# Gate and up by one level of Strassen's scheme, down in four parts, score products in pairs

## The chip, the cores and the metric

The kernel runs on one core of one Trainium2 chip. The metric is the device time of one execution in microseconds, the median over several. The engines are TensorE (matrix products; PE in the profile, PEld its weight loads), VectorE (DVE), ScalarE (ACT), GpSimd (POOL) and SyncE (SP), which issues the loads. DMA engines move data between memory and the on-chip buffers.

## The reference

Four feed-forward layers, one attention and one gating mixer (gMLP) act on x of 512 tokens by 1024, in float32:

```
def _swiglu_ffn(x, w_gate_up, w_down):
    g, u = jnp.split(x @ w_gate_up, 2, axis=-1)
    return (jax.nn.silu(g) * u) @ w_down
...
    for i in range(DEPTH):                       # DEPTH = 2, D_FF = 2816
        x = x + 0.5 * _swiglu_ffn(_rmsnorm(x, ffn1_norm[i]), ffn1_w_gate_up[i], ffn1_w_down[i])
        h = _rmsnorm(x, mix_norm[i])
        # i = 0: x = x + _diff_attention(h, ...)   8 heads of two components, 64 wide
        # i = 1: x = x + _chunked_sgu(h, ...)
        x = x + 0.5 * _swiglu_ffn(_rmsnorm(x, ffn2_norm[i]), ffn2_w_gate_up[i], ffn2_w_down[i])
```

## The kernel before

x stays on the chip as eight tiles of 128 features by 512 tokens (k = 0 to 7). The feed-forward layers are f0 to f3, the norms n0 to n5; the order is f0, attention, f1, f2, gMLP, f3. A float32 product is made of three float32r products (`mm3`, L126 to L129): each operand is split into a high half (ScalarE's copy, L122 for weights) and a low half (VectorE's subtraction, L123), and high times high, high times low and low times high are added in one bank.

A feed-forward layer has 22 tiles of 128 hidden features, in two halves of 11. For a tile one load brings 1 MB (gate and up, 256 columns for each k), two splits of 1024 columns follow, and 8 k times 2 sides times 3 products of 512 tokens fill two banks. The normalisation is applied behind the products: x is only multiplied by the norm's gain (L158, L159), and the row `rb` of 1/rms multiplies the banks in `gated` (L235 to L243), which then takes silu on ScalarE, multiplies, and splits the result into the tiles hh and hl. `rb` is made by `norm.rstd` and `norm.rows` from sums that TensorE takes during the first tile (in f0 the second). After 11 tiles `down` runs: for each of the eight output tiles m one load of 704 KB, two splits, 33 products, and x[m] += 0.5 times the bank (L285). In the second half each finished x[m] goes at once into the next norm.

Four buffers hold weights that are loaded or being loaded in feed-forward and mixers alike (`wraw` two of 2048 columns, `wsplit` five pairs of 1024). A scheduler orders each engine's instructions by need and cost; attention and gMLP first put their tasks in order by a planner of their own (`interleave`), with due times. In attention the score products of a head and row (L495) come in two components of 64 features, each with its own bank, three products and a mask product (L499); they are spread between the products of values (v0p and on).

Of the kernel before, what the change touches and what calls it, by code (L numbers as in the profile page):

```python
# [43 lines left out]
DOWN_CUT = 6  # L44
O_BUFS = 4
U_BUFS = 4
QK_BUFS = 5
BANKS = {"pp": 4, "ps": 3, "po": 1}
HOP = 0.2
# [4 lines left out]
def kernel(  # L54
# [28 lines left out]
    wraw = ctx.enter_context(tc.tile_pool(name="wraw", bufs=2))  # L83
    wsplit = ctx.enter_context(tc.tile_pool(name="wsplit", bufs=5))
# [7 lines left out]
    xh = [acts.tile([P, S], F32R, name=f"xh{k}") for k in range(KT)]  # L92
    xl = [acts.tile([P, S], F32R, name=f"xl{k}") for k in range(KT)]
# [49 lines left out]

    class Norm:


        def __init__(self, layer, kind, name):
            self.g0 = C_GAIN + (layer * 3 + kind) * KT
            self.name = name
            self.acc = stat.tile([P, S], F32, tag="sqacc", name=name + "acc", bufs=1)  # L150

# [17 lines left out]
        def rstd(self):  # L169

            ps = bank(self.name + "ss", "po")
            for n in range(NT):
                nc.tensor.matmul(
                    ps[:, n:n + 1], self.acc[:, n * P:(n + 1) * P], ones[:, 0:1], start=True, stop=True
                )
# [4 lines left out]
        def rows(self, r):  # L180
# [6 lines left out]
            for part, half in ((f32(rh), "h"), (rl, "l")):  # L187
# [37 lines left out]

    def ffn(layer, which, norm, nxt):
        f = layer * 2 + which
        nm = f"f{f}"
        with ExitStack() as c:
            hp = c.enter_context(tc.tile_pool(name=nm + "h", bufs=1, reuse_waits="tile"))  # L230
            tp = c.enter_context(tc.tile_pool(name=nm + "t", bufs=2, reuse_waits="tile"))

            def gated(j, jj, ps):
                gt = tp.tile([P, S], F32, tag="gt", name=f"{nm}g{j}")
                nc.vector.tensor_tensor(gt, ps[0], rb, op=ALU.mult)  # L235
                nc.scalar.activation(gt, gt, AF.Silu)
                ut = tp.tile([P, S], F32, tag="ut", name=f"{nm}u{j}")
                nc.vector.tensor_tensor(ut, ps[1], rb, op=ALU.mult)
# [620 lines left out]
```

## Time and profile before

| | |
|---|---|
| median of 3 runs | 1996.73 us (1996.42 to 1997.2) |
| profiled execution | 1996.96 us, its span 1995.2 us |
| TensorE busy | 1984.2 us, 99%, 9034 products |
| its weight loads | 1629.9 us, 82% |
| VectorE busy | 1032.3 us, 52% |
| ScalarE busy | 670.0 us, 34% |
| DMA | 190.34 MB, mean 95 GB/s |

Busy is the time in which an engine has at least one instruction in work; products overlap, so a product's duration is longer than the step from its start to the next one's. What an instruction costs a full engine is therefore read as the step between starts.

### The profile page before, as it was taken

What the parts mean: (1) busy time and instruction counts of PE and PEld (TensorE: products, weight loads), DVE (VectorE), ACT (ScalarE), POOL (GpSimd) and SP (SyncE); (2) the same over time, 40 slices, a digit from 0 to 9 for tenths busy, and PEclk for the clock granted to TensorE, in tenths of its full rate; (3) what the DMA queues carried; (4) which work ended last, traced back from release to release, by engine and by line L of the source; (5) the groups of instructions that cost most, each with busy time, mean ns of one, the idle gap of its engine ahead of it and who ended that gap; (6) DMA issues with size and microseconds to landing.
All of it is one profiled execution on the core that took longest, in us unless ns stands there. A gap on an engine that the chain in (4) does not pass through costs nothing.

```text
span 1995.2 us, 22193 instructions
## 1 busy us (share of the span) xinstructions
PE 1984.2 (99%) x9034; PEld 1629.9 (82%) x9034; DVE 1032.3 (52%) x1663; ACT 670.0 (34%) x960; POOL 2.6 (0%) x11
## 2 busy tenths in 40 slices
PE   8999999999999999999999999999999999999999
PEld 7888888877778888888888888888888888888887
DVE  7433444567778443444544334445586564434442
ACT  5222323355554322222423223233333242222321
POOL 0000000000000000000000000000000000000000
PEclk9999999999999999999999999999999999999999
DMA  5223222211112222322322232234332222223222
GB/s 193 99 73 120 100 86 94 105 64 64 55 52 85 89 81 95 126 84 74 127 87 90 88 127 85 79 103 146 115 116 85 89 102 88 83 94 127 85 78 81
DMA packets 32934, 190.34 MB, mean 95 GB/s; under 512 B 3776, under 2 KB 4160, under 8 KB 16576
## 3 DMA queue, kind: packets, MB, share of 16 engines
q1 hardware_dynamic: 32832, 188.93, 27.0%
q8 instruction: 71, 1.16, 0.2%
q14 instruction: 31, 0.25, 0.0%
HBM read 186.82 MB, written 2.10 MB: 95 GB/s over the span
## 4 chain that ended last, share of the span: by engine, by line
PE 98%; DVE 1%; ACT 1%; DMA 0%; SPq 0%; issue 0%; ACTq 0%
PE f2p L127 4%; PE f3p L127 4%; PE f3p L128 4%; PE f2p L129 4%; PE f3p L129 4%; PE f2p L128 4%; PE f1p L127 4%; PE f1p L128 4%; PE f1p L129 4%; PE f0p L127 4%; PE f0p L129 4%; PE f0p L128 4%; PE f3dp L127 2%; PE f2dp L129 2%; PE f1dp L127 2%; PE f0dp L129 2%
## 5 line engine op out<-in xcount | busy, mean ns | idle before, releaser
L235 DVE TENSOR_TENSOR f3g<-f3p,n5rbs 128x512 f32<-128x512 f32 x22 | 15.2, 691 | 58.7 <-PE f3p L129 58.7
L235 DVE TENSOR_TENSOR f1g<-f1p,n2rbs 128x512 f32<-128x512 f32 x22 | 15.2, 692 | 58.7 <-PE f1p L129 57.3
L235 DVE TENSOR_TENSOR f2g<-f2p,n3rbs 128x512 f32<-128x512 f32 x22 | 15.2, 691 | 58.7 <-PE f2p L129 58.7
L235 DVE TENSOR_TENSOR f0g<-f0p,n0rbs 128x512 f32<-128x512 f32 x22 | 15.2, 691 | 55.5 <-PE f0p L129 55.5
L158 ACT ACTIVATE xh<-x,sm 128x512 fp32r<-128x512 f32 x48 | 34.3, 718 | 17.8 <-DVE x L750 9.7
L159 DVE SCALAR_TENSOR_TENSOR xl<-x,sm,xh 128x512 fp32r<-128x512 f32 x48 | 35.6, 746 | 8.5 <-ACT xh L158 8.4
L285 DVE SCALAR_TENSOR_TENSOR x<-f3dp,x 128x512 f32<-128x512 f32 x16 | 11.1, 692 | 40.3 <-PE f3dp L129 40.3
L285 DVE SCALAR_TENSOR_TENSOR x<-f2dp,x 128x512 f32<-128x512 f32 x16 | 11.1, 692 | 29.3 <-PE f2dp L129 29.3
L285 DVE SCALAR_TENSOR_TENSOR x<-f1dp,x 128x512 f32<-128x512 f32 x16 | 11.1, 692 | 29.3 <-PE f1dp L129 29.3
L285 DVE SCALAR_TENSOR_TENSOR x<-f0dp,x 128x512 f32<-128x512 f32 x16 | 11.1, 692 | 29.3 <-PE f0dp L129 29.3
L750 DVE TENSOR_TENSOR x<-gop,x 128x512 f32<-128x512 f32 x24 | 16.5, 689 | 18.4 <-PE gop L129 18.4
L242 ACT ACTIVATE f3hh<-f3u 128x512 fp32r<-128x512 f32 x22 | 13.9, 633 | 28.1 <-DVE f3u L239 28.1
L242 ACT ACTIVATE f2hh<-f2u 128x512 fp32r<-128x512 f32 x22 | 13.9, 632 | 28.0 <-DVE f2u L239 28.0
L243 DVE TENSOR_TENSOR f3hl<-f3u,f3hh 128x512 fp32r<-128x512 f32 x22 | 15.2, 692 | 15.4 <-ACT f3hh L242 15.4
L243 DVE TENSOR_TENSOR f2hl<-f2u,f2hh 128x512 fp32r<-128x512 f32 x22 | 15.2, 692 | 15.4 <-ACT f2hh L242 15.4
L242 ACT ACTIVATE f1hh<-f1u 128x512 fp32r<-128x512 f32 x22 | 13.9, 632 | 27.3 <-DVE f1u L239 27.3
L243 DVE TENSOR_TENSOR f1hl<-f1u,f1hh 128x512 fp32r<-128x512 f32 x22 | 15.2, 692 | 14.7 <-ACT f1hh L242 14.7
L242 ACT ACTIVATE f0hh<-f0u 128x512 fp32r<-128x512 f32 x22 | 13.9, 632 | 26.5 <-DVE f0u L239 26.5
L593 DVE TENSOR_TENSOR x<-aop,x 128x512 f32<-128x512 f32 x32 | 21.5, 684 | 2.4 <-PE aop L129 2.3
L243 DVE TENSOR_TENSOR f0hl<-f0u,f0hh 128x512 fp32r<-128x512 f32 x22 | 15.2, 692 | 14.1 <-ACT f0hh L242 14.0
L730 ACT ACTIVATE gh<-gut 128x512 fp32r<-128x512 f32 x16 | 10.1, 631 | 33.7 <-DVE gut L729 33.7
L689 DVE TENSOR_TENSOR gut<-gup,n4rbs 128x512 f32<-128x512 f32 x16 | 11.0, 685 | 13.4 <-PE gup L129 13.4
(3643 smaller groups left out, 6456.7 us busy)
## 6 DMA issues: line engine op xcount, KB each, us to landing
f1gu<-in_gate_up_dram SPq DMA_DIRECT2D x22, 1024.0 KB, 4.8
f2gu<-in_gate_up_dram SPq DMA_DIRECT2D x22, 1024.0 KB, 4.8
f3gu<-in_gate_up_dram SPq DMA_DIRECT2D x22, 1024.0 KB, 4.8
f0gu<-in_gate_up_dram SPq DMA_DIRECT2D x21, 1024.0 KB, 4.8
f0d<-in_down_dram SPq DMA_DIRECT2D x16, 704.0 KB, 4.0
f1d<-in_down_dram SPq DMA_DIRECT2D x16, 704.0 KB, 4.0
f2d<-in_down_dram SPq DMA_DIRECT2D x16, 704.0 KB, 4.1
f3d<-in_down_dram SPq DMA_DIRECT2D x16, 704.0 KB, 4.1
```

Of the source, the lines that this page charges most:

```text
L127: nc.tensor.matmul(ps, sh, mh, start=start, stop=False)
L128: nc.tensor.matmul(ps, sh, ml, start=False, stop=False)
L129: nc.tensor.matmul(ps, sl, mh, start=False, stop=stop)
L158: nc.scalar.activation(xh[k], x[k], AF.Copy, scale=g)
L159: nc.vector.scalar_tensor_tensor(xl[k], x[k], g, f32(xh[k]), op0=ALU.mult, op1=ALU.subtract)
L235: nc.vector.tensor_tensor(gt, ps[0], rb, op=ALU.mult)
L242: nc.scalar.activation(a, ut, AF.Copy)
L243: nc.vector.tensor_tensor(b, ut, f32(a), op=ALU.subtract)
L285: nc.vector.scalar_tensor_tensor(x[m], pt, 0.5, x[m], op0=ALU.mult, op1=ALU.add)
L593: nc.vector.tensor_tensor(x[m], pt, x[m], op=ALU.add)
L689: nc.vector.tensor_tensor(ut, ps, rr["rb"], op=ALU.mult)
L750: nc.vector.tensor_tensor(x[m], pt, x[m], op=ALU.add)
```

## The change

Tiles are taken in pairs, i and i + 11. Tiles 0, 11, 1 and 12 stay as they were (PLAIN = 2); the other nine pairs are done by one level of the Winograd form of Strassen's scheme over (first or second tile) by (first or second half of k) by (first or second 256 tokens): seven products of half the k and half the tokens instead of eight. Each product is done for gate (a) and for up (b), so a pair has 14 turns of 4 k times 3 products of 256 columns, in the order of `turns`, on three accumulators X, Y, Z for each side; `keep` holds what is copied out between.

The weights are four quarters, each a load of 512 KB: a, b (tiles i and i + 11, first half of k), d, c (the same, second half). VectorE makes t = a + b, then t + c once t is split for Q5; two more sums are made by DMAs from GpSimd's queue that load a quarter from memory a second time and add it into the buffer: b += c as soon as t is made, t += d as soon as t + c is split for P6. The last, t + d + c, is split for Q4. All seven weight operands are split as before. `scaled` makes the seven combinations of x once per layer, now with gain and `rb` both multiplied in, and splits them.

Down takes its 22 hidden tiles in four parts (CHUNKS), each when its pairs are done, with two loads and one split of up to 768 columns for each m, and adds to x[m] four times. All products of a feed-forward layer are kept in the program's order. Each norm's xh and xl come from a pool shared with the hidden tiles. Attention has 4 instead of 5 buffers for q and k, gMLP 3 instead of 4 for u, and the score products of a group, save the first, and their masks are kept in program order, the two components alternating.

```diff
-U_BUFS = 4
-QK_BUFS = 5
+U_BUFS = 3
+QK_BUFS = 4
...
+HT = S // 2
+PLAIN = 2
+C_BUFS = 1
+CHUNKS = ((0, 1, 2), (3, 4, 5), (6, 7, 8), (9, 10))
...
+    pairs = ctx.enter_context(tc.tile_pool(name="pairs", bufs=10))
+    wraw = ctx.enter_context(tc.tile_pool(name="wraw", bufs=4))
+    wsplit = ctx.enter_context(tc.tile_pool(name="wsplit", bufs=4))
     psum = ctx.enter_context(tc.tile_pool(name="psum", bufs=8, space=bass.MemoryType.PSUM))
...
+    fixed = []
+
+    def matmul(ps, stationary, moving, start, stop, more=False):
+
+        mm = nc.tensor.matmul(ps, stationary, moving, start=start, stop=stop, skip_group_check=more)
+        if fixed:
+            tc.keep_in_program_order(mm)
+
+    def mm3(ps, sh, sl, mh, ml, start, stop, more=False):
...
+    class Weigh:
+        def __init__(self, pool, srcs, name):
+            self.name, self.done, self.srcs = name, {}, srcs
+            self.raw = {}
+            for q in "abdc":
+                if q == "c":
+                    t = pool.tile([P, 1024], F32, tag="c", name=f"{name}c", bufs=C_BUFS)
+                else:
+                    t = wraw.tile([P, 1024], F32, tag="raw", name=f"{name}{q}")
+                self.raw[q] = t
+                nc.sync.dma_start(t, srcs[q])
+            t = self.raw["t"] = pool.tile([P, 1024], F32, tag="t", name=f"{name}t", bufs=2)
+            nc.vector.tensor_tensor(t, self.raw["a"], self.raw["b"], op=ALU.add)
+            self.more("b", "c")
+        def more(self, to, by):
+            nc.gpsimd.dma_start(self.raw[to], self.srcs[by], accum_op=ALU.add)
+        def take(self, prod):
+            if prod not in self.done:
+                src = {"P1": "a", "Q5": "t", "P6": "t", "P7": "b", "P2": "d", "Q3": "c", "Q4": "t"}[prod]
+                self.done[prod] = split(self.raw[src], D, self.name + prod)
+                if prod == "Q5":
+                    t = self.raw["t"]
+                    nc.vector.tensor_tensor(t, t, self.raw["c"], op=ALU.add)
+                elif prod == "P6":
+                    self.more("t", "d")
+            return self.done[prod]
...
+        slot = {"P1": 0, "P2": 1, "Q4": 2, "Q5": 3, "P6": 4, "P7": 5, "Q3": 6}
+        turns = ["P1a", "P1b", "Q5a", "P6a", "P6b", "Q5b", "P7a", "P7b", "P2a", "P2b", "Q3a", "Q3b", "Q4a", "Q4b"]
...
+            def gated(j, ps):
+                h = room(f"{nm}r{j}")
+                g, u = h[:, :2, :], h[:, 2:4, :]
+                nc.vector.tensor_tensor(g, two(ps[0]), two(rb), op=ALU.mult)
+                nc.scalar.activation(g, g, AF.Silu)
+                nc.vector.tensor_tensor(u, two(ps[1]), two(rb), op=ALU.mult)
+                nc.vector.tensor_tensor(u, u, g, op=ALU.mult)
+                late_halves.append((j, u))
+            def scaled(kp):
+                h = room(f"{nm}x{kp}")
+                for k, dst in ((kp, h[:, 0:8:7, :]), (kp + 4, h[:, 1:3, :])):
+                    nc.vector.scalar_tensor_tensor(
+                        dst, two(x[k]), norm.gain(k), two(rb), op0=ALU.mult, op1=ALU.mult
+                    )
+                nc.vector.tensor_tensor(h[:, 3, :], h[:, 7, :], h[:, 2, :], op=ALU.subtract)
+                nc.vector.tensor_tensor(h[:, 4, :], h[:, 3, :], h[:, 0, :], op=ALU.subtract)
+                nc.vector.tensor_tensor(h[:, 5, :], h[:, 0, :], h[:, 7, :], op=ALU.subtract)
+                nc.vector.tensor_tensor(h[:, 6, :], h[:, 1, :], h[:, 4, :], op=ALU.add)
+                hi, lo = (
+                    fp.tile([P, 7, HT], F32R, tag="x" + q, name=f"{nm}x{kp}{q}", bufs=4) for q in "hl"
+                )
+                nc.scalar.activation(hi, h[:, :7, :], AF.Copy)
+                nc.vector.tensor_tensor(lo, h[:, :7, :], f32(hi), op=ALU.subtract)
+                xf.append((hi, lo))
+            late_halves = []
+            plain = [j for i in range(PLAIN) for j in (i, i + FH)]
...
+                late.append((j, ps))
+                if at == 1:
+                    for unit in late:
+                        gated(*unit)
+                    late = []
+            for kp in range(4):
+                scaled(kp)
+            for unit in late:
+                gated(*unit)
+            for unit in late_halves:
+                halves_of(*unit)
+            def gate_up_pair(i):
+                quarter = lambda j, q: gate_up[f, j][:, q * D:(q + 1) * D]
+                weigh = Weigh(
+                    fp, {"a": quarter(i, 0), "b": quarter(i + FH, 0), "c": quarter(i + FH, 1), "d": quarter(i, 1)},
+                    f"{nm}w{i}",
+                )
+                h = room(f"{nm}r{i}")
+                g, h = h[:, :4, :], h[:, 4:, :]
+                keep, acc = {}, {}
+                for turn in turns:
+                    prod, u = turn[:2], turn[2]
+                    wh, wl = weigh.take(prod)
+                    home = {"P2": "Z", "Q4": "X"}.get(prod, {"P": "X", "Q": "Y"}[prod[0]])
+                    fresh = prod in ("P1", "P2", "Q5")
+                    if fresh:
+                        acc[home + u] = bank(f"{weigh.name}{home}{u}", "ps" if home == "X" else "pp")
+                    ps = acc[home + u][:, :HT]
+                    for k, (hi, lo) in enumerate(xf):
+                        c0 = slice((k * 2 + (u == "b")) * P, (k * 2 + (u == "b") + 1) * P)
+                        mm3(
+                            ps, wh[:, c0], wl[:, c0], hi[:, slot[prod], :], lo[:, slot[prod], :],
+                            fresh and k == 0, k == 3, not fresh,
+                        )
+                    out = g if u == "a" else h
+                    if prod in ("P1", "P6", "P7"):
+                        if prod == "P1":
+                            keep[u] = fp.tile([P, 2, HT], F32, tag="keep" + u, name=f"{nm}k{i}{u}")
+                        if prod == "P7":
+                            kept = fp.tile([P, HT], F32, tag="keep", name=f"{nm}k{i}{u}")
+                        else:
+                            kept = keep[u][:, ("P1", "P6").index(prod), :]
+                        nc.scalar.activation(kept, ps, AF.Copy)
+                    if prod == "P7":
+                        nc.vector.tensor_tensor(out[:, 3, :], acc["Y" + u][:, :HT], kept, op=ALU.subtract)
+                    elif prod == "P2":
+                        nc.vector.tensor_tensor(out[:, 0, :], ps, keep[u][:, 0, :], op=ALU.add)
+                        if u == "a":
+                            nc.scalar.activation(g[:, 0, :], g[:, 0, :], AF.Silu)
+                        else:
+                            nc.vector.tensor_tensor(h[:, 0, :], h[:, 0, :], g[:, 0, :], op=ALU.mult)
...
+            def down_part(chunk):
+                k0, n = chunk[0], len(chunk)
+                js = [i + q * FH for q in range(2) for i in chunk]
...
+            for i in range(PLAIN, FH):
+                gate_up_pair(i)
+                for chunk in CHUNKS[:-2]:
+                    if i == chunk[-1] + 1:
+                        down_part(chunk)
+            down_part(CHUNKS[-2])
+            down_part(CHUNKS[-1])
+            fixed.pop()
...
-                        nc.tensor.matmul(
+                        mm = nc.tensor.matmul(
                             pss[cc][:, :L], qT[a][c0, i * P:L], kT[b][c0, :L], start=(a + b == 0), stop=False
                         )
+                        if a + b + cc > 0:
+                            tc.keep_in_program_order(mm)
                 for cc in range(2):
-                    nc.tensor.matmul(pss[cc][:, i * P:L], ident_b, mask_b, start=False, stop=True)
+                    tc.keep_in_program_order(
+                        nc.tensor.matmul(pss[cc][:, i * P:L], ident_b, mask_b, start=False, stop=True)
+                    )
                 for cc in range(2):
```

VectorE at the entry of f1, before. f1g and f1u are the two sides of a gated tile, f1w31l the low half of a weight split, n2rbs the norm row.

```order
L235 TENSOR_TENSOR f1g_5349<-f1p_5267,n2rbs 128x512 [waits Activation_49]
L238 TENSOR_TENSOR f1u_5352<-f1p_5268,n2rbs 128x512
L239 TENSOR_TENSOR f1u_5352<-f1u_5352,f1g_5349 128x512 [waits DVE_49,Activation_49]
L123 TENSOR_TENSOR f1w31l<-f1gu_5499,f1w31h 128x1024 [waits PE_49,Activation_49]
L243 TENSOR_TENSOR f1hl_5356<-f1u_5352,f1hh_5355 128x512 [waits Activation_49]
L235 TENSOR_TENSOR f1g_5419<-f1p_5369,n2rbs 128x512 [waits PE_49]
L238 TENSOR_TENSOR f1u_5422<-f1p_5370,n2rbs 128x512 [waits PE_49]
L123 TENSOR_TENSOR f1w40l<-f1gu_5569,f1w40h 128x1024 [waits DMAHW0_49,Activation_49]
```

VectorE at the same place after the norm row, now: f1x are the combinations of x, x1 to x3 those of k pairs 1 to 3, f1w2 the first pair's weights, f1r the gating of a plain tile.

```order
L325 SCALAR_TENSOR_TENSOR f1x_6737<-x_84,sm,n2rbs 128x512
L330 TENSOR_TENSOR f1x_6737<-f1x_6737 128x256 [waits DVE_49]
L328 TENSOR_TENSOR f1x_6737<-f1x_6737 128x256 [waits DVE_49]
L273 TENSOR_TENSOR f1w2t<-f1w2t,f1w2c 128x1024 [waits DMAHW7_49]
L336 TENSOR_TENSOR f1x2l<-f1x_6726,f1x2h 128x1792 [waits Activation_49]
L329 TENSOR_TENSOR f1x_6737<-f1x_6737 128x256 [waits DVE_49]
L315 TENSOR_TENSOR f1r_6748<-f1p_6592,n2rbs 128x512 [waits DVE_49]
L331 TENSOR_TENSOR f1x_6737<-f1x_6737 128x256 [waits DVE_49]
L317 TENSOR_TENSOR f1r_6748<-f1p_6593,n2rbs 128x512
L126 TENSOR_TENSOR f1w2P6l<-f1w2t,f1w2P6h 128x1024 [waits PE_49,Activation_49]
L318 TENSOR_TENSOR f1r_6748<-f1r_6748 128x512 [waits DVE_49,Activation_49]
L336 TENSOR_TENSOR f1x3l<-f1x_6737,f1x3h 128x1792 [waits Activation_49]
```

Where only gating and weight splits stood, the combinations of x, the sum of two weight quarters and the gating of plain tiles now stand in turn, and the low half of the last combination (x3l) comes last.

VectorE in one pair of f2 with the next one's start, now (f2w4 and f2w5 are pairs, DMASW2 the accumulating DMA into t, Y and Z accumulators).

```order
L126 TENSOR_TENSOR f2w4P7l<-f2w4b,f2w4P7h 128x1024 [waits DMASW0_49,Activation_49]
L126 TENSOR_TENSOR f2w4P2l<-f2w4d,f2w4P2h 128x1024 [waits DMAHW0_49,PE_49,Activation_49]
L126 TENSOR_TENSOR f2w4Q3l<-f2w4c,f2w4Q3h 128x1024 [waits PE_49,Activation_49]
L126 TENSOR_TENSOR f2w4Q4l<-f2w4t,f2w4Q4h 128x1024 [waits DMASW2_49,PE_49,Activation_49]
L406 TENSOR_TENSOR f2r_10942<-f2w4Ya,f2k4a 128x256 [waits Activation_49]
L126 TENSOR_TENSOR f2w5P1l<-f2w5a,f2w5P1h 128x1024 [waits PE_49,Activation_49]
L406 TENSOR_TENSOR f2r_10942<-f2w4Yb,f2k4b 128x256 [waits Activation_49]
L408 TENSOR_TENSOR f2r_10942<-f2w4Za,f2k4a 128x256 [waits PE_49]
L408 TENSOR_TENSOR f2r_10942<-f2w4Zb,f2k4b 128x256 [waits PE_49]
```

The split for Q4 waits for the accumulating DMA; behind it on VectorE stand the outputs of Y (L406), of Z (L408) and the split for the next pair's first product.

TensorE at a score group of head 0, 256 columns, before: one component (a0s) with its mask, then the values' products (v0p).

```order
L495 MATMUL a0s_2863<-qk0Th_2792,qk0Th_2783 128x256 [waits DVE_49]
L495 MATMUL a0s_2863<-qk0Tl_2793,qk0Th_2783 128x256
L495 MATMUL a0s_2863<-qk0Th_2792,qk0Tl_2784 128x256
L499 LDWEIGHTS ident_b
L499 MATMUL a0s_2863<-mask_b,ident_b 128x128
L127 MATMUL v0p_2726<-av01s0h,xh_86 128x512
L128 MATMUL v0p_2726<-av01s0l,xh_86 128x512
```

The other component's four follow only after nine more products of v0p. The same place now, from the last of the v0p products between (a0s with the lower number is the first component).

```order
L133 MATMUL v0p_3845<-av01s0h,n1x5l 128x512
L659 MATMUL a0s_3988<-qk0Th_3914,qk0Th_3905 128x256 [waits Activation_49]
L659 MATMUL a0s_3987<-qk0Tl_3915,qk0Th_3905 128x256
L659 MATMUL a0s_3988<-qk0Tl_3915,qk0Th_3905 128x256
L659 MATMUL a0s_3987<-qk0Th_3914,qk0Tl_3906 128x256
L659 MATMUL a0s_3988<-qk0Th_3914,qk0Tl_3906 128x256
L666 LDWEIGHTS ident_b
L666 MATMUL a0s_3987<-mask_b,ident_b 128x128
```

The first component's first product still stands by itself, twelve products of v0p ahead; its other two now alternate with the second component's three.

## Rows read from the trace of the kernel before

**Rows 1.** The page: busy time of each engine, the chain by engine, the clock

```profile
PE 1984.2 (99%) x9034; PEld 1629.9 (82%) x9034; DVE 1032.3 (52%) x1663; ACT 670.0 (34%) x960; POOL 2.6 (0%) x11
...
PEclk9999999999999999999999999999999999999999
...
PE 98%; DVE 1%; ACT 1%; DMA 0%; SPq 0%; issue 0%; ACTq 0%
```

**Rows 2.** Stretches: attention, layer f2. us, length, busy of engines, PEclk, DMA share, GB/s

```profile
386.00:640.00 254.00, 253.13 (x1327) 195.63 (x1327) 193.31 (x557) 140.64 (x288) 0.00 (x0) 1.00 0.17 60
...
999.00:1370.00 371.00, 371.00 (x1640) 307.27 (x1641) 167.07 (x212) 109.45 (x139) 1.09 (x1) 1.00 0.29 102
```

**Rows 3.** Timeline of TensorE in f0: start, duration, engine, line, operation, output<-inputs

```profile
299.84 0.39 PE L127 MATMUL f0p<-xh,f0w210h 128*128 128x512 f32 x1
...
302.56 0.39 PE L127 MATMUL f0p<-xh,f0w210h 128*128 128x512 f32 x1
```

**Rows 4.** Timeline of TensorE: score products of 256 columns, first and last pair

```profile
407.03 0.28 PE L495 MATMUL a0s<-qk0Tl,qk0Th 64*128 64x256 f32 x1
407.15 0.28 PE L495 MATMUL a0s<-qk0Th,qk0Tl 64*128 64x256 f32 x1
...
574.85 0.28 PE L495 MATMUL a7s<-qk3Tl,qk3Th 64*128 64x256 f32 x1
574.97 0.28 PE L495 MATMUL a7s<-qk3Th,qk3Tl 64*128 64x256 f32 x1
```

**Rows 5.** Timeline of TensorE: twelve products of 128 columns in one run

```profile
512.99 1.47 PE L469 MATMUL qk2t<-ident,qk2n 128*128 128x128 f32 x12
```

**Rows 6.** Timeline of VectorE: widths 1024, 512, 512 with scalar, 256

```profile
1028.46 1.23 DVE L123 TENSOR_TENSOR f2w50l<-f2gu,f2w50h 128x1024 fp32r<-128x1024 f32 x1 [0.23 <-ACT f2w50h L122]
1029.60 0.69 DVE L239 TENSOR_TENSOR f2u<-f2u,f2g 128x512 f32<-128x512 f32 x1
...
34.24 0.68 DVE L238 TENSOR_TENSOR f0u<-f0p,n0rbs 128x512 f32<-128x512 f32 x1
34.84 0.68 DVE L235 TENSOR_TENSOR f0g<-f0p,n0rbs 128x512 f32<-128x512 f32 x1
...
11.53 1.41 DVE L159 SCALAR_TENSOR_TENSOR xl<-x,sm,xh 128x512 fp32r<-128x512 f32 x2
...
397.74 1.09 DVE L458 TENSOR_TENSOR qk0n<-qk0n,qk0rq 128x256 f32<-128x256 f32 x3
```

**Rows 7.** Timeline: the norm row of f0, product and copy

```profile
31.43 0.39 PE L195 MATMUL n0rb<-n0dgh,ones_r 128*128 128x512 f32 x1
...
32.37 0.58 ACT L199 ACTIVATE n0rbs<-n0rb 128x512 f32<-128x512 f32 x1
```

**Rows 8.** DMA issues: tile, queue, count, KB each, median us from issue to landing

```profile
f1gu<-in_gate_up_dram SPq DMA_DIRECT2D x22, 1024.0 KB, 4.8
...
f0d<-in_down_dram SPq DMA_DIRECT2D x16, 704.0 KB, 4.0
...
gv00r<-in_w_gv_dram SPq DMA_DIRECT2D x1, 1024.0 KB, 6.2
```

**Rows 9.** Timeline of TensorE: one score group of one component between other products

```profile
412.20 0.40 PE L128 MATMUL v0p<-av01s0l,xh 128*128 128x512 f32 x1
412.55 0.50 PE L495 MATMUL a0s<-qk0Th,qk0Th 64*128 64x512 f32 x1
412.89 0.39 PE L495 MATMUL a0s<-qk0Tl,qk0Th 64*128 64x512 f32 x1
413.12 0.39 PE L495 MATMUL a0s<-qk0Th,qk0Tl 64*128 64x512 f32 x1
413.44 0.23 PE L499 MATMUL a0s<-mask_b,ident_b 128*128 128x128 bf16 x1
413.48 0.48 PE L129 MATMUL v0p<-av01s0h,xl 128*128 128x512 f32 x1
413.80 0.40 PE L127 MATMUL v0p<-av01s0h,xh 128*128 128x512 f32 x1
```

More of the change, by code (lines that the diff above doesn't have):

```diff
@@ L142, in rsqrt, with half_pair @@
         return y
+    def half_pair(name):
+        return tuple(pairs.tile([P, S], F32R, tag=q, name=name + q) for q in "hl")
     class Norm:
@@ L202, in begin @@
     def begin(norm):
-        raw = wraw.tile([P, 2048], F32, tag="raw", name="w0")
+        raws = [wraw.tile([P, 1024], F32, tag="raw", name=f"w0{q}") for q in range(2)]
         cuts = [(0, 1), (1, 2), (2, 4), (4, 6), (6, 8)]
@@ new lines, in ffn, with room, two, halves_of @@
+            fixed.append(1)
+            fp = c.enter_context(tc.tile_pool(name=nm + "p", bufs=1, reuse_waits="tile"))
+            def room(name):
+                return fp.tile([P, 8, HT], F32, tag="room", name=name, bufs=2)
+            def two(t):
+                return t.rearrange("p (a b) -> p a b", a=2)
+            hidden = {}
+            def halves_of(j, u):
+                hi, lo = hidden[j] = half_pair(f"{nm}h{j}")
+                nc.scalar.activation(two(hi), u, AF.Copy)
+                nc.vector.tensor_tensor(two(lo), u, f32(two(hi)), op=ALU.subtract)
@@ new lines, in ffn @@
+            late_halves = []
+            plain = [j for i in range(PLAIN) for j in (i, i + FH)]
+            held = []
+            for at, j in enumerate(plain):
+                if first and at == 0:
+                    parts = begin(norm)
+                else:
+                    parts = [
+                        split(load(gate_up[f, j][:, q * D:(q + 1) * D], f"{nm}gu{j}{q}"), D, f"{nm}w{j}{q}")
+                        for q in range(2)
+                    ]
+                ps = [bank(f"{nm}p{j}{u}", "ps" if first and at == 1 else "pp") for u in range(2)]
+                for k in range(KT):
+                    wh, wl = parts[k // 4]
+                    for u in range(2):
+                        c0 = slice((k % 4 * 2 + u) * P, (k % 4 * 2 + u + 1) * P)
+                        mm3(ps[u], wh[:, c0], wl[:, c0], norm.xh[k], norm.xl[k], k == 0, k == KT - 1)
+                    if rb is None and at == first:
+                        if k == 3:
+                            r = norm.rstd()
+                        elif k == KT - 1:
+                            rb = norm.rows(r)
+                late.append((j, ps))
[3 more added lines that the diff above has]
+                    late = []
@@ new lines, in down_part @@
+            def down_part(chunk):
+                k0, n = chunk[0], len(chunk)
+                js = [i + q * FH for q in range(2) for i in chunk]
+                for m in range(KT):
+                    raw = wraw.tile([P, 1024], F32, tag="raw", name=f"{nm}d{k0}{m}")
+                    for q in range(2):
+                        nc.sync.dma_start(raw[:, q * n * P:(q + 1) * n * P], down[f, q, m][:, k0 * P:(k0 + n) * P])
+                    wh, wl = split(raw, 2 * n * P, f"{nm}dw{k0}{m}")
+                    pt = bank(f"{nm}dp{k0}{m}", "pp")
+                    for k, j in enumerate(js):
+                        c0 = slice(k * P, (k + 1) * P)
+                        mm3(pt, wh[:, c0], wl[:, c0], hidden[j][0], hidden[j][1], k == 0, k == 2 * n - 1)
```

129 lines of the change are left out of this document (46 added, 83 removed).

## The prediction

> **What bounds the kernel now.** I read the page's shares first: TensorE is busy for 99% of the span, and the chain that ended last runs through it for 98%, at full clock (2.4 GHz) throughout [rows 1]. Then the stretches: in a whole feed-forward layer TensorE has no idle time, VectorE works 167 of 371 us (45%) and the DMA engines are 29% used [rows 2]. So only what shortens TensorE's list, or starves it, can change the time. Third, the timeline: in a feed-forward layer 512-column products start every (302.56 − 299.84)/12 = 0.2267 us [rows 3], each with a weight load of its own that is hidden. The sum below is made against the profiled execution's 1996.96 us (span 1995.2 and 1.8 around it); the median of the runs is 1996.73, the same for this purpose. A measurement of this kernel tells 0.2%, 4 us, from no change.
>
> **Term 1, the products of gate and up.** A pair of f tiles (i and i+11) takes 2 tiles x 8 k x 2 sides x 3 split products = 96 products of 512 columns, 96 x 0.2267 = 21.76 us. As Strassen pair it is 14 turns (7 products, gate and up) x 4 k pairs x 3 = 168 products of 256 columns. What a 256-column step costs decides the change: break-even is 21.76/168 = 0.1295 us. The feed-forward layers have none, but the attention scores do: on half of the rows, with the same kind of weight load, the second and third product of a group start 0.12 us apart (407.03 and 407.15, to 574.85 and 574.97); of 16 such steps four read 0.11 and twelve 0.12, mean 0.1175 [rows 4]. From below: half of the 512 step, 0.1133, or, further down, the step of the 128-column products, twelve in 1.47 us, 0.11 to 0.12 each though the columns are a quarter: there the weight load no longer hides [rows 5]. From above: all that the 512 step has beyond 512 columns at 2.4 GHz stays whole, 0.2267 − 0.1067 = 0.120. I take 0.1175, a measured row: 168 x 0.1175 = 19.74 us, 2.02 less per pair; 9 pairs in each of 4 layers make 36 pairs: **−73 us** (−98 at 0.1133, −58 at 0.120).
>
> The Trainium skill, "TensorE: Matmul & The Clock Gate", section "Back-to-back issue gap", gives columns/2.4 GHz + 2.5 ns when warm, so an estimate of 0.109 us for 256 columns, and its section "LDWEIGHTS" gives 0.107 us for a load whatever the columns. By that term 1 would be −124 us. For 512 columns the rule says 0.216 and the rows 0.2267 [rows 3], so the rows decide; the rule stands as a rival below.
>
> **Term 2, the entry into the pairs.** Every layer first needs x in seven combinations, made from the finished norm row on VectorE. VectorE's steps from start to start: 1024 wide 1.14 us (1028.46 to 1029.60), 512 wide 0.60 (34.24 to 34.84), 512 wide with scalar 0.70 (two in 1.41), 256 wide 0.36 (three in 1.09) [rows 6]; 1792 wide, not in the trace, is 1.14 + 768 x (1.14 − 0.60)/512 = 1.95. One `scaled` is 2 x 0.70 + 4 x 0.36 + 1.95 = 4.8. From the end of the second plain tile to the last operand x3l, the order of f1 holds: four `scaled` 19.2, four splits 4.6, the sum t + c 1.1, the gating of one tile 2.4 and most of another's 1.8: 29.1 us. TensorE's cover is the two plain tiles left, 96 x 0.2267 = 21.8, and the nine products of P1a that don't need x3, 1.06: 22.8. So it waits 6.3 us, in f1, f2 and f3. In f0 the norm row comes a tile later: its copy starts at 32.37 and takes 0.58, against an end of the tile's products at 31.43 [rows 7], 1.5 later; one more tile is gated (2.4), and a split and t = a + b (2.3) stand behind instead of ahead: 29.1 + 6.2 − 22.8 = 12.5. Sum 3 x 6.3 + 12.5 = **+31 us**. Bounds: +15 if the scheduler's order leaves less in front of x3l, +45 if each low half also waits for its high half on ScalarE. None of this is on the path today.
>
> **Term 3, a pair in steady state.** VectorE: seven splits and two sums 9 x 1.14, eight 256-wide outputs x 0.36, three 512-wide x 0.60: 15.0 us of 19.7, 4.7 over: 0. ScalarE, which works two thirds of VectorE's time now [rows 1], gets fewer of the steps. Cover gone, each 0.1 us per pair is 3.6 us.
>
> The two accumulating DMAs are what the trace doesn't show. b += c has time: it starts when t = a + b is done in the pair before, and P7 is the seventh turn. t += d is tight: it may start when P6 has been split from t, about 2.5 us into the pair, and Q4's split on VectorE stands ahead of the outputs that free Y for Q3a, the eleventh turn of 12 x 0.1175 = 1.41 us, at 14.1 us. Behind Q4l come L406, P1l and L406 (with it 3.1 us), ahead of it ScalarE's split (1): 14.1 − 3.1 − 1 − 2.5 = 7.5 us allowed from issue to landing. From below: a plain 512 KB load. 1024 KB land in 4.8 us, 704 KB in 4.0 [rows 8], so 512 KB in 3.5, of which 1.3 are transfer. An accumulate reads its target too, so up to three times the transfer, 6.1; queued behind one more load 7.4. From above: twice a 1024 KB landing, 9.6. I take 6: 0. At 9.6 it is 2.1 late; VectorE's slack takes half of that, 18 us for each us over 36 pairs: +38. Past 10 us each further us costs 36.
>
> **Term 4, scores.** A group of one component between full-row products costs its three steps and, from the rows, entry 0.35 − 0.23, first step 0.34 − 0.23, mask 0.32 − 0.23, return 0.32 − 0.23: 0.41 us [rows 9]. In the order before, 20 of 32 (head, row) groups have the two components apart; after, the second component's three steps run beside the first's last two, but in 27 of 32 the first's first product stays apart, by itself. So 0.82 + 6 steps become 0.71 + 4 steps: 0.33 to 0.56 us less, 8.5 in all; of 12 groups that stood together 7 lose about 0.44, 3. **−5 us** (−14 to +3).
>
> **Nothing.** Down has the same 48 x 11 products a layer; a chunk of three gives VectorE at most 8 x (1.14 + 0.70) = 14.7 of 32.6 us. The fewer buffers of attention and gMLP: 0 (to +4); TensorE waits 0.9 us in 254 of attention now [rows 2]. SP issues 547 transfers instead of 228, off the path.
>
> **Sum.** 1996.96 − 73 + 31 − 5 = **1950 us**.
>
> **Rivals.**
> (a) *The accumulates are late*, at the split of Q4. For it: nothing in the trace adds in flight, loads share the 16 engines, already 29% used [rows 2], and one 1024 KB load took 6.2 instead of 4.8 [rows 8]. Against: 7.5 us are twice a plain 512 KB landing. From 7.5 us it costs, at about 10 (the gain of 47 us spent) it decides: at 11 us 1950 + 45 + 36 = 2031, slower. Chance 0.15, two thirds of it slower than before. The Trainium skill, "DMA: Bandwidth & Descriptors", section "Issuing engines are not separate DMA queues", says that transfers issued from GpSimd run on the same 16 engines as the others; that speaks for this rival, and no run shown yet has any.
> (b) *A 256-column step is only the weight load's floor*, the 0.11 of the 128-column steps [rows 5]. Against: rows 4 themselves. 168 x 0.11 = 18.5: 1996.96 − 36 x (21.76 − 18.5) + 31 − 5 = 1906; chance 0.04. The Trainium skill's rule above comes to the same. At half the 512 step, 0.1133, it is 1925, inside the forecast's range.
> (c) *The change doesn't give fewer TensorE microseconds*: with full rows the load doesn't hide under 256 columns, and a step is 0.13 or more, as the 0.34 instead of 0.23 of a group's first step hints [rows 9]. Against: the steps of rows 4. At 0.135, 168 x 0.135 = 22.7: 1996.96 + 33 + 26 = 2056; chance 0.03.
> (d) *VectorE starves a pair*: it has 4.7 us of 19.7 over, in bursts. If TensorE waits 1 us in each pair, 1986; chance 0.08. For: the order puts P2, Q3 and Q4 splits ahead of outputs, so one late split blocks the outputs; against: wh and wl have four buffers each, three products ahead.
>
> **Numbers.** Forecast 0.70, its own range 1924 to 1978; (a) 0.15, (b) 0.04, (c) 0.03, (d) 0.08. Range 1916 to 1996. Faster by over 0.2%: 0.70 + 0.04 + 0.07 + a quarter of (a) = 0.84; slower 0.10 of (a) + 0.03 = 0.13; the rest, 0.03, within.
>
> **What will show it.** Step of the 256-column products 0.117; in each layer TensorE idle about 6 us (12 in f0) before and in the first P1a, with VectorE's x3l as releaser; afterwards no idle time; accumulates landing in about 6 us, Q4's split never the releaser of a TensorE wait; VectorE some 75% busy in pairs; attention about 5 us shorter. I am wrong if TensorE waits every pair, or if the step is not between 0.113 and 0.121.

## The result, and the profile after

The changed kernel takes 1972.45 us (median of 4 runs, 1971.33 to 1973.43), before 1996.88; the ratio is 0.9878 [0.9861, 0.9895]. Forecast were 1950 and a range of 1916 to 1996: faster, as said, by 24 us instead of 47. The profiled execution has a span of 1969.6 us.

The page after, busy time, granted clock, the accumulating DMAs' queue, the chain by engine (beside [rows 1]):

```profile
PE 1935.8 (98%) x11626; PEld 1712.2 (87%) x11626; DVE 1327.3 (67%) x2127; ACT 879.0 (45%) x1336; POOL 65.1 (3%) x83
...
PEclk9899999999999999999999999999999999999999
...
q0 software_dynamic: 10368, 37.75, 11.5%
...
PE 92%; DVE 6%; issue 1%; ACT 1%; DMA 0%; SPq 0%
```

TensorE still sets the time, but the chain now goes through VectorE for 6%, and in one slice (49 to 98 us, with f0's entry into the pairs) the clock isn't full. What each stage gained, the starts of its first product in the two traces say (us; the forecast is the prediction's 9 x 2.02 a layer, less its entry):

| stage | before | after | difference | forecast |
|---|---|---|---|---|
| f0 | 363.97 | 359.83 | -4.1 | -5.7 |
| attention | 263.15 | 259.67 | -3.5 | -5 |
| f1 | 360.93 | 357.77 | -3.2 | -11.9 |
| f2 | 360.47 | 352.46 | -8.0 | -11.9 |
| gMLP | 277.02 | 277.23 | +0.2 | 0 |
| f3 | 364.49 | 357.40 | -7.1 | -11.9 |

The timeline of f1, columns as in [rows 3]: the first Strassen pair's first product, its waits, slow products, its last product, then the second pair's first and last.

```profile
674.01 0.28 PE L133 MATMUL f1w2Xa<-f1x0h,f1w2P1h 128*128 128x256 f32 x1
...
674.96 0.28 PE L133 MATMUL f1w2Xa<-f1x2h,f1w2P1l 128*128 128x256 f32 x1
676.17 1.68 ACT L335 ACTIVATE f1x3h<-f1x 128x1792 fp32r<-128x1792 f32 x1
677.90 0.41 PE L133 MATMUL f1w2Xa<-f1x3h,f1w2P1h 128*128 128x256 f32 x1 [2.66 <-ACT f1x3h L335]
678.13 2.02 DVE L336 TENSOR_TENSOR f1x3l<-f1x,f1x3h 128x1792 fp32r<-128x1792 f32 x1
680.20 0.58 PE L133 MATMUL f1w2Xa<-f1x3l,f1w2P1h 128*128 128x256 f32 x1 [1.89 <-DVE f1x3l L336]
...
681.01 0.41 PE L133 MATMUL f1w2Xb<-f1x0l,f1w2P1h 128*128 128x256 f32 x1
681.22 0.41 PE L133 MATMUL f1w2Xb<-f1x0h,f1w2P1l 128*128 128x256 f32 x1
...
701.22 0.28 PE L133 MATMUL f1w2Xb<-f1x3h,f1w2Q4l 128*128 128x256 f32 x1
701.34 0.28 PE L133 MATMUL f1w3Xa<-f1x0h,f1w3P1h 128*128 128x256 f32 x1
...
721.38 0.28 PE L133 MATMUL f1w3Xb<-f1x3h,f1w3Q4l 128*128 128x256 f32 x1
```

The second pair has 167 steps in 721.38 - 701.34 = 20.04 us: 0.120 each. All later pairs of the four layers read the same, but one (below). The first pair takes 27.21 us. It waits for x3h on ScalarE and x3l on VectorE, and after that a step is 0.21. The stretches around it (columns as in [rows 2]) show why:

```profile
676.00:681.00 5.00, 1.21 (x4) 0.99 (x5) 5.00 (x6) 2.48 (x3) 0.86 (x1) 0.71 0.33 40
681.00:684.00 3.00, 3.00 (x16) 3.00 (x16) 2.68 (x4) 1.42 (x4) 0.00 (x0) 0.50 0.55 108
684.00:688.00 4.00, 4.00 (x31) 4.00 (x31) 2.96 (x3) 1.82 (x3) 0.00 (x0) 0.88 0.62 179
688.00:692.00 4.00, 4.00 (x36) 4.00 (x35) 2.24 (x2) 2.78 (x4) 0.86 (x1) 1.00 0.73 139
```

From about 678, still in the wait, the granted clock is 0.50, TensorE's lower level of 1.2 GHz, until about 685: 16 products in 3 us where 25 would go. What TensorE waited for (us in total, times, longest; the program's start, which the kernel before has too, and smaller ones left out):

```profile
PE f1w2Xa L133 <- ACT f1x3h L335: 2.7, 1, 2.7
...
PE n2ss L133 <- DVE n2acc L188: 2.5, 1, 2.5
PE f0w2Xa L133 <- ACT f0x3h L335: 2.4, 1, 2.4
PE f0w2Xa L133 <- DVE f0x2l L336: 2.3, 1, 2.3
```

f2 and f3 have the same row, and each of the three 1.8 or 1.9 us more for x3l. n2ss, the products that sum n2's squares in f1, is a wait that the prediction does not have:

```profile
632.02 0.68 DVE L188 TENSOR_TENSOR n2acc<-n2acc,n2sq 128x512 f32<-128x512 f32 x1
632.85 1.02 PE L133 MATMUL n2ss<-ones,n2acc 128*128 128x1 f32 x8 [2.47 <-DVE n2acc L188]
```

Before, n2ss stood 37 products into the layer's list; kept in program order it stands after 24, ahead of the last n2acc. In the accumulating DMAs (columns as in [rows 8]) there is one outlier:

```profile
f1w9t<-in_gate_up_dram POOLq DMA_DIRECT2D x1, 512.0 KB, 9.2
...
f2w4b<-in_gate_up_dram POOLq DMA_DIRECT2D x1, 512.0 KB, 5.5
f2w4t<-in_gate_up_dram POOLq DMA_DIRECT2D x1, 512.0 KB, 5.5
```

The rest land in 5.3 to 7.6 us. The pair with 9.2 is the one that reads 20.23 instead of 20.04 us.

### The profile page after: what moved, and what is told of

It is laid out like the page before. It is cut to its first block, busy times and chain, and to the rows that moved or that the text cites. A ratio compares the mean times of both kernels' runs of the same rounds, so it can differ in the third digit from the quotient of the medians.

```text
span 1969.6 us, 29451 instructions
## 1 busy us (share of the span) xinstructions
PE 1935.8 (98%) x11626; PEld 1712.2 (87%) x11626; DVE 1327.3 (67%) x2127; ACT 879.0 (45%) x1336; POOL 65.1 (3%) x83
## 4 chain that ended last, share of the span: by engine, by line
PE 92%; DVE 6%; issue 1%; ACT 1%; DMA 0%; SPq 0%
PE f3dp L133 6%; PE f0dp L133 6%; PE f2dp L133 6%; PE f1dp L133 6%; PE gup L133 4%; PE gop L133 4%; PE aop L133 2%; PE v1p L133 1%; PE qk2p L133 1%; PE v0p L133 1%; PE qk1p L133 1%; PE qk0p L133 1%; PE gv0p L133 1%; PE gv1p L133 1%; PE gv2p L133 1%; PE gv3p L133 1%
## 5 line engine op out<-in xcount | busy, mean ns | idle before, releaser
L439 DVE SCALAR_TENSOR_TENSOR x<-f3dp,x 128x512 f32<-128x512 f32 x32 | 22.1, 691 | 60.2 <-PE f3dp L133 60.2
L439 DVE SCALAR_TENSOR_TENSOR x<-f0dp,x 128x512 f32<-128x512 f32 x32 | 22.1, 690 | 49.1 <-PE f0dp L133 49.1
L439 DVE SCALAR_TENSOR_TENSOR x<-f2dp,x 128x512 f32<-128x512 f32 x32 | 22.1, 690 | 49.1 <-PE f2dp L133 49.1
L439 DVE SCALAR_TENSOR_TENSOR x<-f1dp,x 128x512 f32<-128x512 f32 x32 | 22.1, 690 | 48.9 <-PE f1dp L133 48.9
L888 PEld LDWEIGHTS gs<-wT,gv 128*128 128x128 f32 x128 | 16.1, 191 | 0.9
L893 DVE TENSOR_TENSOR gst<-gs,bs 128x512 f32<-128x512 f32 x16 | 11.0, 687 | 8.8 <-PE gs L888 8.8
L888 PE MATMUL gs<-wT,gv 128*128 128x128 f32 x128 | 16.2, 274 | 0.0
L858 ACT ACTIVATE gut<-gut,sm 128x512 f32<-128x512 f32 x16 | 11.5, 721 | 6.7 <-DVE gut L857 6.5
L873 DVE SCALAR_TENSOR_TENSOR gv<-gv,lnmv,lng 128x512 f32<-128x512 f32 x16 | 11.5, 741 | 1.6 <-DMA lng<-in_ln_g_dram 1.6
L874 DVE SCALAR_TENSOR_TENSOR gv<-gv,lny,lnb 128x512 f32<-128x512 f32 x16 | 11.6, 746 | 1.1 <-DMA lnb<-in_ln_b_dram 1.1
L416 ACT ACTIVATE f0r<-f0r 128x512 f32<-128x512 f32 x9 | 5.7, 633 | 14.3 <-DVE f0r L414 14.3
L416 ACT ACTIVATE f3r<-f3r 128x512 f32<-128x512 f32 x9 | 5.7, 633 | 14.3 <-DVE f3r L414 14.3
L416 ACT ACTIVATE f2r<-f2r 128x512 f32<-128x512 f32 x9 | 5.7, 633 | 14.3 <-DVE f2r L414 14.3
```

The lines of the kernel that those rows point to most:

```text
L416: nc.scalar.activation(g[:, 2:, :], g[:, 2:, :], AF.Silu)
L439: nc.vector.scalar_tensor_tensor(x[m], pt, 0.5, x[m], op0=ALU.mult, op1=ALU.add)
L858: nc.scalar.activation(ut, ut, AF.Gelu, bias=sm[:, C_BU + c:C_BU + c + 1])
L873: nc.vector.scalar_tensor_tensor(vv, vv, mv[:, n, 0:1], gr, op0=ALU.subtract, op1=ALU.mult)
L874: nc.vector.scalar_tensor_tensor(vv, vv, rr["y"][:, n:n + 1], lr, op0=ALU.mult, op1=ALU.add)
L888: nc.tensor.matmul(ps[:, n * P:(n + 1) * P], v32[n][:, c * P:(c + 1) * P], wT[:, g, :], start=True, stop=True)
```

## The experiments

**The step.** Runs of 24 products behind the kernel's last one:

```diff
             down_part(CHUNKS[-1])
+            if nxt is None:
+                probe = bank("probe", "po")
+                for n in (128, 192, 256, 320, 384, 448, 512):
+                    for i in range(24):
+                        matmul(probe[:, :n], hidden[10][0][:, i % 4 * P:(i % 4 + 1) * P], hidden[21][0][:, :n], True, True)
...
```

> The kernel after, with runs of 24 products on 128 rows behind its last product (columns 128, 192, 256, 320, 384, 448, 512, each with changing weights, then 256 with one and the same weights); their bank is read by nobody. Question: why a 256-column step is 0.120 us in the pairs where 0.1175 was forecast. Theory A, a fixed part: each product costs its columns at 2.4 GHz and 13.3 ns more, whatever its columns (512: 0.2267, 256: 0.120), down to the 0.112 of the 128-column products. Then 320: 0.147, 384: 0.173, 448: 0.200, 192: 0.112. Theory B, a floor: 0.120 is what a product with a load on 128 rows costs at least; then 192 and 128 read 0.120 too. If the fixed part comes from changing the weights, the run with one weight reads 0.107, otherwise 0.120.

The timeline (each row is one run; the last begins behind its first product):

```profile
1965.86 2.79 PE L133 MATMUL probe<-f3h21h,f3h10h 128*128 128x128 f32 x24
1968.49 2.87 PE L133 MATMUL probe<-f3h21h,f3h10h 128*128 128x192 f32 x24
1971.20 3.06 PE L133 MATMUL probe<-f3h21h,f3h10h 128*128 128x256 f32 x24
1974.10 3.69 PE L133 MATMUL probe<-f3h21h,f3h10h 128*128 128x320 f32 x24
1977.62 4.33 PE L133 MATMUL probe<-f3h21h,f3h10h 128*128 128x384 f32 x24
1981.78 5.12 PE L133 MATMUL probe<-f3h21h,f3h10h 128*128 128x448 f32 x24
1986.74 5.65 PE L133 MATMUL probe<-f3h21h,f3h10h 128*128 128x512 f32 x24
...
1992.34 2.92 PE L133 MATMUL probe<-f3h21h,f3h10h 128*128 128x256 f32 x23
```

From start to start by 24, for 128 to 448 columns: 0.110, 0.113, 0.121, 0.147, 0.173, 0.207 us. Theory A holds from 256 columns on: columns at 2.4 GHz and 13 ns (20 at 448, which it does not explain); 128 and 192 columns read a floor of 0.11. The 13 ns don't come from changing the weights: with one and the same, (2.92 - 0.28)/22 = 0.120. There too the trace has a weight load for each product, so what they are is not shown. The Trainium skill, "TensorE: Matmul & The Clock Gate", section "Back-to-back issue gap", has 2.5 ns for the part beyond the columns; here it is five times that, and the measurement decides.

**The clock.**

```diff
+                        if i == PLAIN and turn == "P1a" and k == 3:
+                            idle = bank(f"{nm}idle", "po")
...
+                            fill(22)
+                            matmul(ps, wh[:, c0], hi[:, slot[prod], :], False, False)
+                            fill(17)
+                            matmul(ps, wh[:, c0], lo[:, slot[prod], :], False, False)
```

> The kernel after, with products that nobody reads (22 and 17 of 256 columns, 2.64 and 2.04 us) put into P1a of each layer's first pair, just where TensorE waits 2.94 us for x3h and 2.29 us for x3l. Theory: half of what the entry costs beyond its idle time is the clock, which falls to 1.2 GHz in the wait; with TensorE at work there the first pair of f2 and f3 shrinks from 26.4 and 27.1 us to about 25.3 (20.04 and the 5.2 of the wait itself), in all 4 to 6 us less, 1967. Rival: the clock falls for another reason (the change of shape from 512 to 256 columns): the slow products stay, time 1972 to 1974.

Measured 1966.5 (1963.79 to 1968.09), ratio 0.9845 [0.9831, 0.986]. The same stretches of f1:

```profile
676.00:681.00 5.00, 4.96 (x41) 4.76 (x40) 5.00 (x8) 3.39 (x4) 0.86 (x1) 1.00 0.08 8
681.00:684.00 3.00, 3.00 (x26) 2.93 (x25) 3.00 (x5) 1.40 (x4) 0.00 (x0) 1.00 0.94 161
```

26 products instead of 16, at full clock; the first pairs of f1, f2 and f3 take 25.13 us each (f0's, where TensorE still waits for x2, 29.87). The shapes change as before and the clock stays full: here it is the idle time that brings the low clock.

**The entry: cover, order, both.** One more plain pair (the edit is PLAIN = 3):

> The kernel after with PLAIN = 3: one more pair of tiles done plainly ahead of the first Strassen pair in each layer, 43.5 us more cover for the combinations of x. Theory: the four waits at the entry (first pairs of 30.55, 27.21, 26.36, 27.14 instead of 20.04 us, in sum 31.1) are VectorE's list and go whole; four pairs lose 1.6 us each: 1972.5 - 31.1 + 6.4 = 1948. Rival: the first pair is slow for its own reason (accumulating DMAs just begun, clock), whatever comes ahead: 1972.5 + 6.4 = 1979.

1972.08, ratio 0.9874 [0.9859, 0.9889]: neither. The first Strassen pair waits no more, but the fifth plain tile does:

```profile
PE f0p L133 <- DVE f0r L315: 6.3, 1, 6.3
...
PE f1p L133 <- DVE f1r L315: 1.9, 1, 1.9
...
PE f1p L133 <- DVE f1r L317: 1.1, 1, 1.1
```

L315 and L317 are the gating of an earlier plain tile (in f1 to f3 the third), which frees the banks for the fifth; it stood behind the combinations. I had counted x3l as the end of VectorE's list and not asked what else is in it that TensorE needs. So, with PLAIN = 3, the order was changed as well:

```diff
                         elif k == KT - 1:
                             rb = norm.rows(r)
+                            for unit in late:
+                                gated(*unit)
+                            late = []
+                            scaled(0)
                 late.append((j, ps))
-                if at == 1:
+                if rb is not None:
                     for unit in late:
                         gated(*unit)
                     late = []
-            for kp in range(4):
-                scaled(kp)
-            for unit in late:
-                gated(*unit)
+                    if len(xf) < 4:
+                        scaled(len(xf))
```

> The kernel after with PLAIN = 3 and another order in the entry: each plain tile is gated as soon as it is done, and one of the four combinations of x follows it (the first right behind the norm row), instead of all four ahead of the gating of the later tiles. With PLAIN = 3 alone the time stayed at 1972, since TensorE waited 2.26 and 1.5 us in each layer at its fifth plain tile for the gating (L315, L317) that frees its banks and stood behind the combinations. Theory: with the gating first nothing waits; each of 32 pairs saves 1.6 us, 51 in all, attention 3.5, and the wait for n2's sum (5 with its slow clock) stays: 1997 - 51.2 - 3.5 + 5 + 1 = 1948. Rival: VectorE has no room in this stretch in any order, the wait goes to the first pair or the plain tiles' weight splits: 1960 to 1972.

1948.61, ratio 0.9756 [0.9743, 0.9769]: the theory's number. No wait in an entry is left but the one for n2's sum, 2.5 us. And the order with PLAIN = 2:

> The kernel after with the other order in the entry (each plain tile gated as soon as it is done, one combination of x behind each), and PLAIN = 2 as it was: with PLAIN = 3 this order gave 1948.6, PLAIN = 3 without it 1972.1. Question: is it the order or the cover that counts? Theory: both are needed, since from the norm row to x3l VectorE has four combinations (19.2), four gatings (9.6) and seven or eight weight steps of 1.14, some 37 us, against three plain tiles of 10.9 that are left, 32.7; 4 to 6 us of wait stay in each layer, with their slow products: 1968 to 1976. Rival: in the kernel after, the combinations only began too late (VectorE idle for some 8 us behind the norm row); with the order the wait is gone and no pair is given up: 1997 - 57.6 - 3.5 + 5 = 1941 to 1945.

1975.75, ratio 0.9892 [0.9875, 0.9908]: with two plain pairs the waits stay (f2 3.8 us, f0 14.3). Cover alone and order alone give nothing, both together 24 us.

**n2's sum later, the version that beats both.** On top of PLAIN = 3 and the order:

```diff
-                    if rb is None and at == first:
-                        if k == 3:
+                    if rb is None:
+                        if (at, k) == ((0, 5) if f == 1 else (first, 3)):
                             r = norm.rstd()
-                        elif k == KT - 1:
+                        elif (at, k) == ((1, 1) if f == 1 else (first, KT - 1)):
```

> The same (PLAIN = 3, gating first), and in f1 the sum of squares of n2 is taken 12 products later (after the sixth k instead of the fourth), its norm row in the second tile. Theory: TensorE's wait of 2.86 us there is the fixed place of these products ahead of n2acc, 2.7 us later n2acc is there; with it go the wait and the slow products behind it, 5 us at most: 3 to 5 less than with the order alone, 1943 to 1945. Rival: the later norm row makes the entry of f1 late by as much, and nothing is won: 1948.

1944.22 (1943.61 to 1944.67), ratio 0.9735 [0.9722, 0.9748]. Its busy time, and its waits:

```profile
PE 1931.0 (99%) x11338; PEld 1694.2 (87%) x11338; DVE 1305.2 (67%) x2095; ACT 858.4 (44%) x1296; POOL 58.2 (3%) x75
```

```profile
PE f0p L133 <- ACT w00wh L237: 6.2, 2, 5.5
PE n2rb L133 <- DVE n2dgh L208: 0.6, 1, 0.6
PE f0p L133 <- DVE w00wl L238: 0.4, 1, 0.4
PE a4s L661 <- ACT a4e L680: 0.4, 1, 0.4
```

Besides the program's start no wait is longer than 0.6 us. It takes 4.4 us less than with cover and order, all of them in f1 (353.59 to 349.19), where n2's sum stands. f2 is 12.74 us shorter than before, and 8 pairs x 1.60 are 12.8.

**The sums on VectorE instead of DMAs.**

```diff
-            nc.gpsimd.dma_start(self.raw[to], self.srcs[by], accum_op=ALU.add)
+            nc.vector.tensor_tensor(self.raw[to], self.raw[to], self.raw[by], op=ALU.add)
```

> The kernel after with all four weight sums on VectorE: the two accumulating DMAs are replaced by additions of 1024 columns from the buffers that hold the quarters. Theory: the accumulates land in 5.3 to 6.1 us against 7.5 allowed, so they cost nothing now, and VectorE has 4.7 us of a pair over, of which the two additions take 2.3: pairs after the first stay at 20.04 us; at the entry, where TensorE waits for VectorE, one or two additions stand ahead of x3l: 1.1 to 2.3 more in each layer, 1976 to 1982. Rival: VectorE then starves the pairs in bursts: 1 us in each of 32 pairs, 2010. Rival: the accumulates do cost something hidden (shared transfer engines, loads that land late): faster than 1968.

1973.74, ratio 0.9884 [0.9868, 0.9901], which can't be told from the change itself. The pairs stay at 20.04; the first pair grows by 1.1 us in f0 and by 0.1 to 0.2 in the others, where 1.1 to 2.3 were expected. The accumulating DMAs cost nothing and earn next to nothing.

**An accumulate of twice the length.** t += d goes out twice, so d is added twice and the result is another one:

```diff
                     self.more("t", "d")
+                    self.more("t", "d")
```

> The kernel after with the accumulating DMA t += d issued twice in a row, so that d is added twice into the weight sum of Q4 (that changes what is computed). Landing goes from 5.5 to about 11 us. Theory of the prediction: 7.5 us are allowed, half of what is beyond is taken by VectorE's slack to 10, from there all counts, 18 x 2.5 + 36 x 1 = 81: 2053, with Q4's split as VectorE's releaser and TensorE waiting for Y in nearly every pair; more if the next pair's b += c is held up behind it on GpSimd. Rival: there is more room than the 7.5 us that were worked out (Q4 is the last product), and the time stays within 1972 to 1985.

2086.5 (2083.55 to 2093.22), ratio 1.0453 [1.0435, 1.0471]. Two waits of TensorE, two of VectorE, and the two accumulates of one pair with the split behind them:

```profile
PE f0w8Ya L133 <- DVE f0r L407: 7.1, 1, 7.1
PE f2w5Ya L133 <- DVE f2r L407: 6.6, 1, 6.6
```

```profile
DVE f0w8Q4l L126 <- ACT f0w8Q4h L125: 10.4, 1, 10.4
DVE f2w5Q4l L126 <- ACT f2w5Q4h L125: 9.9, 1, 9.9
```

```profile
1190.24 0.86 POOL L264 DMA_DIRECT2D f2w5t<-in_gate_up_dram  x1 [1.21 <-ACT f2k5a L405]
1196.89 0.86 POOL L264 DMA_DIRECT2D f2w5t<-in_gate_up_dram  x1 [5.79 <-DMA f2w5t<-in_gate_up_dram]
...
1205.51 1.06 ACT L125 ACTIVATE f2w5Q4h<-f2w5t 128x1024 fp32r<-128x1024 f32 x1 [9.80 <-DMA f2w5t<-in_gate_up_dram]
```

Rival (a) as told: Q4's split late, the outputs of Y (L407 here, L406 in the change) behind it, TensorE waiting for Y. It is 33 us worse than the forecast. The second accumulate goes out only when the first has landed, so from the first issue to the last landing it is 13.0 us in the median of the 36 pairs (11.2 to 15.7), not 11. In all 32 pairs behind the first of a layer TensorE's wait for Y is what that landing lies beyond 11.6 us behind the pair's first product: 84 us in sum. The other 30 us that these pairs grow are slow products behind the waits (clock 0.973 over the whole run).

**The scores.** Their order set free as before (no `keep_in_program_order` for products and masks):

> The kernel after with the score products and masks in no kept order, as before. Theory: the trace after shows the products of the two components, on 64 rows each, starting 1 to 4 ns apart, two at a time; without it attention goes back from 259.7 to about 263 us: 1972.5 + 3.5 = 1976. Rival: attention's 3.5 us come from the buffers (QK_BUFS, 512 KB loads), and the time stays at 1972 to 1973.

1976.11, ratio 0.9896 [0.9882, 0.9909]; attention takes 263.25 us again. In the trace after, one group of 512 columns:

```profile
427.66 0.50 PE L659 MATMUL a1s<-qk0Th,qk0Th 64*128 64x512 f32 x1
427.66 0.73 PE L659 MATMUL a1s<-qk0Tl,qk0Th 64*128 64x512 f32 x2
428.00 0.62 PE L659 MATMUL a1s<-qk0Th,qk0Tl 64*128 64x512 f32 x2
```

Products of the two components start together. With the first one kept too (the condition `a + b + cc > 0` dropped):

> The kernel after with every score product kept in program order, the first of a group too, so that all six of a group stand together, two by two. Theory: in 27 of 32 groups the lone first product costs its step and the change to and from full rows, 0.3 us and more; together it runs beside the other component's: 27 x 0.3 = 8 us less, 1964. Rival: the first product stood alone because its partner's operands or bank come later; kept together both wait, and what is won is lost as idle time: 1970 to 1980.

1971.75, ratio 0.9876 [0.9861, 0.9891], and it tells nothing: TensorE's list came out the same, with 36 stretches of score products as in the change. A kept order holds a product against other kept ones; the v0p products between aren't kept.

**Without Strassen.** All 22 tiles plain, the hidden tiles in a pool of the layer's own, the rest of the change kept:

```diff
-PLAIN = 2
+PLAIN = FH
...
-                if at == 1:
+                if at >= 1:
...
+                for chunk in CHUNKS[:-2]:
+                    if at == 2 * chunk[-1] + 3:
+                        down_part(chunk)
```

> The kernel after with all 22 tiles of gate and up done plainly, and everything else of the change kept (down in four parts, loads of 512 KB, kept order, fewer buffers, score products); the hidden tiles stand in a pool of the layer. Theory: the scheme itself is worth 36 x 1.6 = 57.6 less 31.1 at the entry, so 26.5 us; the rest is nothing but attention's 3.5 less and a wait of n2's sum of squares in f1, 3.9 more: 1972.5 + 26.5 = 1999. Rival: the four parts of down, the smaller loads or the fixed order cost or give something of their own: outside 1995 to 2003.

1997.44 (11 runs, 1996.99 to 1999.39), ratio 1.0005 [0.9996, 1.0014]. In the profiled execution (1999.39) f2 and f3 are within 0.02 us of before, attention 3.6 shorter, f1 5.4 longer: four parts, small loads and kept order cost nothing in themselves, only n2ss's place does. Its wait is 2.5 us here as in the change; behind it the granted clock is 0.50 for 6.8 us here and for 3.4 there, so the place costs 3.9 to 5.4 us by the execution. The scheme by itself is worth 1997.44 - 1972.45 = 25 us.

## Why the prediction was right, and what was off

- **Term 1**: the right mechanism, one size off. The step is 0.120, the upper bound, not 0.1175: 36 x (21.76 - 168 x 0.120) = -57.6 instead of -73. The step that failed is "I take 0.1175, a measured row": that row [rows 4] is of products on 64 rows, whose step at 256 columns is 2 to 3 ns shorter (why is not shown); the 512-column row on 128 rows [rows 3] had the answer, its part beyond the columns being fixed. This is 15 of the 22 us missed. Rivals (b) and (c) fall with it.
- **Term 2**: 31 was forecast, and the first pairs are 10.5, 7.2, 6.3 and 7.1 us longer than the others, 31.1. That the sums agree is luck, for the sum hides two errors: TensorE's waits are 5.0 in f1 to f3 and 8.5 in f0, 23.5 instead of 31 (in f1 x3l is done 27.9 us behind the second plain tile's end, where 29.1 were worked out; the cover is the 22.8 worked out); the slow products behind them, 7.6, were not in the prediction at all. x3l on VectorE releases the last wait, as told; the longer one before it ends with x3h on ScalarE, which the prediction doesn't name.
- **Term 3**: 0 and 0. Accumulates were taken as 6 us and are 5.5. Their limit was put at 7.5 behind an issue at 2.5, so 10 us behind the pair's start, and lies at 11.6 there: the one landing of 9.2 costs 0.19 us, where the prediction's rule gives 0.85. Beyond the limit each us counts whole, and VectorE's slack takes no half of it (the run with the accumulate twice). Rival (a) is real, but 2 to 3 us away; (d) did not happen, VectorE even takes two more sums.
- **Term 4**: -3.5 instead of -5. The components do run side by side, and without the kept order the 3.5 are gone. Why it isn't 5 stays open: the lone first product was counted in the forecast, and the run that should have joined it to the others changed nothing.
- **Nothing**: right for down, buffers and loads (the run without Strassen). Wrong for "kept in program order", which the prediction does not cost: in f1 it puts n2ss ahead of n2acc, 3.9 us with its slow products (f1's -3.2 against f3's -7.1; 4.4 between the last two versions).

The sum from the runs: -57.6 + 31.1 + 3.9 - 3.5 + 0.2 = -25.9; the spans differ by 25.6.

## What to carry to other kernels

Before halving a product's columns, separate what a step has beyond its columns at the full clock: it is paid for each product, so seven eighths of the work in products of half the width cost 0.926 of the time here and not 0.875. Where a setup runs behind other work, list everything on that engine that the next stage needs, the freeing of banks too: cover without the right order gave nothing, nor order without cover. An order that is kept for one purpose also pins what stands among it; look for a product in it whose input comes late.

## What the runs showed of the hardware

- Two waits in a row, with starts 2.94 and 2.29 us apart, brought TensorE to 1.2 GHz for some 3 to 5 us more of work in f1 to f3; a single wait of 2.5 us (n2ss) did it too. Products that nobody reads, put into the entry's waits, kept the clock at 1.00 there and won 6 us.
- Two products on 64 rows each, one component's and the other's, mostly start 3 to 4 ns apart. The Trainium skill, "TensorE: Matmul & The Clock Gate", section "Part 3: Packing small matmuls — row/col tiling", says that products on different row groups run at the same time, about 4 ns apart; the trace agrees.
- A 512 KB accumulating DMA lands in 5.5 us in the median beside 3.6 for a plain load, and VectorE's 1792-wide step is 1.94 us, 1.95 as estimated.
